# Weight sums on VectorE, doubled products in two stages, and attention's later sums in row 0

## The chip, the cores and the metric

The kernel runs on one core of a Trainium2 chip. The metric is device time in microseconds, as the median of several executions; a separate profiled execution gives the trace. TensorE (PE) multiplies matrices into PSUM, which here is split into eight banks of 128 x 512 float32. VectorE (DVE) and ScalarE (ACT) read PSUM and SBUF, GpSimd (POOL) works on SBUF and issues some transfers, SyncE (SP) issues the others. Each engine executes its own list of instructions strictly in order.

## The reference: one layer of a hybrid decoder

There are 512 tokens, a model width of 2048, and float32 throughout.

```
h = RMSNorm(x)
[u | v_sgu | q | k | v_att | g_a | g_b] = h @ W_in            # 2048 x 9216
y_a = gelu(u) * (tril(W_s) v_norm + b)                        # chunks of 128 tokens
y_b = stick-breaking attention, 8 heads of 128, blocks of 128 queries:
      z = q k^T * scale
      log_1m = where(key < query, log_sigmoid(-z), 0)
      tail   = sum of log_1m over the keys that come later
      w      = where(key < query, exp(log_sigmoid(z) + tail), 0);  y_b = w v
x += (sigmoid(g_a) * (y_a W_up_a) + sigmoid(g_b) * (y_b W_up_b)) @ W_o
x += (silu(gate) * up) @ W_ffn_out,   [gate | up] = RMSNorm(x) @ W_ffn_in   # hidden 5632
x += sigmoid(RMSNorm(x) @ W_pg) * (p @ W_ple)
```

## The kernel before

**Numbers.** TensorE's fast format, float32r, keeps fewer bits than float32. So each operand is split into a high and a low part, `hi = round(x)` on ACT (L313 for weights, L245 for activations) and `lo = x - hi` on VectorE (L310, L246). One float32 product is three float32r products: hi by hi, hi by lo, lo by hi. `mm3` issues them as three matmuls (L250, L251, L252).

**Seven products for eight.** Most matrices are multiplied in pairs of tiles: 256 x 256 weights against 256 rows of 512 tokens, seen as 2 x 2 blocks, with Strassen's scheme in Winograd's form ("S" units; "P" units are plain). It takes seven block products of 128 x 128 weights against 256 columns instead of eight. Seven weight blocks are needed: three land as they are, two are made by a transfer that adds while it writes (L317, issued on POOL's queue), and two are sums that POOL makes with two additions (L329) into a small buffer, `summed`.

**Preparing weights.** Class `Weights` does it in four steps for two units at a time: `landed` (the adding transfer), `high` (ACT, L313), `sums` (POOL, L329), `rest` (VectorE's L310, then L313 and L310 for the two sums). Three pairs of buffers `whi`/`wlo` (slots) hold the results and four landing buffers the raw weights. `in_turn` pins the order of these instructions and of the evictions on each engine; the remaining order is set by a list scheduler with its own estimates.

**Pairs.** A `Pair` accumulates one output block of 256 rows x 512 tokens over 8 units, two units at a time. In the first stage (33 of the 36 column blocks of `W_in`, and the attention and the gating beside them) products share banks: the seven halves `a, a, q, q, z, y, y` take four banks, with three 256-column matmuls for each product. In FFN-in (43 of 44 blocks) the pair is *doubled*: the stationary hi block meets [hi | lo] of the activations in one matmul of 512 columns (L589), then the lo block meets hi in one of 256 (L591). Each of the seven products then has a whole bank, hi part and lo part side by side: six banks of the pool `ps` and one of `small`. `mix` or `mix_doubled` evicts them while the last two units run. In `mix_doubled` the seven banks are p1, p6, p7, p5, p4, p2, p3 in the order of the products.

**Attention** runs beside the first stage, two heads per round, four rounds. For each head, and each block j of 128 keys from the last to the first, `stage_a` makes the logits and `stage_b` the sums: a triangular matrix of ones times the block's terms (L987, float32, up to 512 columns), plus all ones times `later`, the running sum of the later blocks (L989, float32). `later` is kept on POOL (L997) and VectorE (L999). L991 subtracts the result.

## Time and profile before

| | us |
|---|---|
| median of 3 runs (lowest, highest) | 2770.14 (2769.76, 2771.31) |
| span of the profiled execution | 2768.0 |
| that execution's time above its span | not recorded; the median lies 2.1 above the span |
| first stage with attention, about 110 to 846 | 736 |
| gated merge with W_up, 846 to 1213 | 367 |
| FFN-in, 1256 to 2109 | 853 |
| FFN-out, 2109 to 2490, and the last gate, 2490 to 2768 | 381 and 278 |

The stage bounds are read from where the lines of a stage begin and end in the trace. A timeline row gives start, duration, engine, line, what is written and read, shapes and count. Matmuls overlap in the pipeline: a matmul of 256 columns lasts 0.28 us in a row, but the next starts much sooner, so the cost of a matmul is the distance between two starts. In a row of grouped instructions the columns are busy time, mean duration of one, and idle time of the engine before them with what ended it. A few per cent of the matmul records are missing, so counts of matmuls are taken from the program.

### The profile page before, as it was taken

What the parts mean: (1) busy time and instruction counts of PE and PEld (TensorE: products, weight loads), DVE (VectorE), ACT (ScalarE), POOL (GpSimd) and SP (SyncE); (2) the same over time, 40 slices, a digit from 0 to 9 for tenths busy, and PEclk for the clock granted to TensorE, in tenths of its full rate; (3) what the DMA queues carried; (4) which work ended last, traced back from release to release, by engine and by line L of the source; (5) the groups of instructions that cost most, each with busy time, mean ns of one, the idle gap of its engine ahead of it and who ended that gap; (6) DMA issues with size and microseconds to landing.
All of it is one profiled execution on the core that took longest, in us unless ns stands there. A gap on an engine that the chain in (4) does not pass through costs nothing.

```text
span 2768.0 us, 46391 instructions
## 1 busy us (share of the span) xinstructions
PE 2709.9 (98%) x17243; PEld 2442.2 (88%) x17243; DVE 1922.3 (69%) x2581; ACT 1351.4 (49%) x2043; POOL 1203.9 (43%) x1321
## 2 busy tenths in 40 slices
PE   8999999999999999999999999999999999999999
PEld 6899999999999889978888888888887998988898
DVE  7565656565666566578788888878888457677766
ACT  7655556564554334365444444444445344444543
POOL 0455555555551012215656656665663323423232
PEclk9999999999999999999999999999999999999999
DMA  7567677667776447667878877887886668787785
GB/s 218 141 169 180 171 174 172 165 173 192 174 181 205 132 144 203 196 205 196 210 196 199 199 196 194 201 200 198 200 193 197 179 167 235 201 258 223 229 227 154
DMA packets 302851, 529.09 MB, mean 191 GB/s; under 512 B 25632, under 2 KB 162848, under 8 KB 302624
## 3 DMA queue, kind: packets, MB, share of 16 engines
q1 hardware_dynamic: 241872, 425.70, 48.7%
q0 software_dynamic: 60752, 100.43, 23.6%
q8 instruction: 135, 2.21, 0.3%
q14 instruction: 92, 0.75, 0.1%
HBM read 478.84 MB, written 47.19 MB: 190 GB/s over the span
## 4 chain that ended last, share of the span: by engine, by line
PE 79%; DVE 8%; DMA 4%; ACT 3%; issue 2%; POOL 2%; SPq 0%; DVEq 0%; ACTq 0%; POOLq 0%
PE ps L251 18%; PE ps L250 18%; PE ps L252 18%; PE ps L589 13%; PE ps L591 7%; DVE out L649 3%; DVE wlo L310 3%; PE small L589 2%; POOL wholes L329 2%; DMA wholes<-x 2%; PE small L591 1%; DMA wholes<-hid 1%; ACT whi L313 1%; DVE wholes L464 1%; DVE parts L246 1%
## 5 line engine op out<-in xcount | busy, mean ns | idle before, releaser
L313 ACT ACTIVATE whi<-wholes 128x512 fp32r<-128x512 f32 (+4 forms) x950 | 854.1, 917 | 975.2 <-POOL wholes L329 350.9
L310 DVE TENSOR_TENSOR wlo<-wholes,whi 128x512 fp32r<-128x512 f32 (+4 forms) x950 | 1039.1, 1117 | 388.0 <-ACT whi L313 384.2
L250 PE MATMUL ps<-parts,whi 128*128 128x256 f32 (+1 forms) x3995 | 1249.0, 315 | 24.9 <-ACT whi L313 13.3
L251 PE MATMUL ps<-parts,whi 128*128 128x256 f32 (+1 forms) x3960 | 1233.7, 312 | 3.4 <-DVE parts L246 3.4
L252 PE MATMUL ps<-parts,wlo 128*128 128x256 f32 (+1 forms) x3960 | 1231.0, 311 | 1.4 <-DVE wlo L310 1.4
L329 POOL TENSOR_TENSOR wholes<-wholes 128x256 f32<-128x256 f32 (+1 forms) x794 | 789.0, 994 | 760.0 <-DVE wlo L310 492.9
L250 PEld LDWEIGHTS ps<-parts,whi 128*128 128x128 f32 x3995 | 765.1, 192 | 74.2 <-ACT whi L313 14.2
L251 PEld LDWEIGHTS ps<-parts,whi 128*128 128x128 f32 x3960 | 759.1, 192 | 49.5 <-DVE parts L246 7.0
L252 PEld LDWEIGHTS ps<-parts,wlo 128*128 128x128 f32 x3960 | 758.3, 192 | 40.6 <-DVE wlo L310 2.5
L589 PE MATMUL ps<-parts,whi 128*128 128x512 f32 x2064 | 736.1, 397 | 7.0 <-DVE out L649 5.6
L591 PE MATMUL ps<-parts,wlo 128*128 128x256 f32 x2064 | 578.4, 280 | 0.0
L589 PEld LDWEIGHTS ps<-parts,whi 128*128 128x128 f32 x2064 | 387.2, 188 | 107.5 <-issue 18.5
L591 PEld LDWEIGHTS ps<-parts,wlo 128*128 128x128 f32 x2064 | 390.4, 189 | 0.0
L317 POOL DMA_DIRECT2D wholes<-w_ffn_in x172 | 152.1, 884 | 252.6 <-DMA wholes<-w_ffn_in 201.6
L317 POOL DMA_DIRECT2D wholes<-w_in x132 | 118.3, 900 | 188.3 <-DMA wholes<-w_in 186.1
L246 DVE TENSOR_TENSOR parts<-wholes,parts 128x1024 fp32r<-128x1024 f32 (+3 forms) x129 | 127.4, 1006 | 22.8 <-ACT parts L245 22.0
L649 DVE TENSOR_TENSOR out<-out,ps 128x256 f32<-128x256 f32 x258 | 106.5, 413 | 45.5 <-ACT out L646 44.7
L618 DVE TENSOR_TENSOR out<-out 128x256 f32<-128x256 f32 x59 | 25.8, 438 | 157.6 <-ACT out L615 157.6
L589 PE MATMUL small<-parts,whi 128*128 128x512 f32 x344 | 130.0, 395 | 0.0
L245 ACT ACTIVATE parts<-wholes 128x1024 fp32r<-128x1024 f32 (+3 forms) x129 | 105.9, 844 | 45.6 <-DMA wholes<-hid 21.3
L317 POOL DMA_DIRECT2D wholes<-w_ffn_out x56 | 57.8, 1043 | 94.0 <-DMA wholes<-w_ffn_out 47.9
L591 PE MATMUL small<-parts,wlo 128*128 128x256 f32 x344 | 96.4, 280 | 0.0
(119 smaller groups left out, 1646.8 us busy)
## 6 DMA issues: line engine op xcount, KB each, us to landing
wholes<-w_ffn_in SPq DMA_DIRECT2D x172, 384.0 KB, 5.1
wholes<-w_in SPq DMA_DIRECT2D x132, 384.0 KB, 4.7
wholes<-w_ffn_in SPq DMA_DIRECT2D x172, 256.0 KB, 4.4
wholes<-w_ffn_in POOLq DMA_DIRECT2D x172, 256.0 KB, 5.4
wholes<-w_in SPq DMA_DIRECT2D x132, 256.0 KB, 3.9
wholes<-w_in POOLq DMA_DIRECT2D x132, 256.0 KB, 4.5
wholes<-x SPq DMA_DIRECT2D x32, 512.0 KB, 5.5
wholes<-w_ffn_out SPq DMA_DIRECT2D x31, 512.0 KB, 3.8
```

What stands on the lines that cost most here:

```text
L245: return (nc.scalar.activation(hi, src, AF.Copy), nc.vector.tensor_tensor(out=lo, in0=src, in1=hi.bitcast(F32), op=ALU.subtract))
L246: nc.vector.tensor_tensor(out=lo, in0=src, in1=hi.bitcast(F32), op=ALU.subtract))
L250: nc.tensor.matmul(ps[:, s], sh, mh[:, s], start=start, stop=False)
L251: nc.tensor.matmul(ps, sh, ml, start=False, stop=False)
L252: return nc.tensor.matmul(ps, sl, mh, start=False, stop=stop)
L310: in_turn(nc.vector.tensor_tensor(out=self.lo[:, blocks], in0=r, in1=h.bitcast(F32), op=ALU.subtract))
L313: in_turn(nc.scalar.activation(h, r, AF.Copy))
L317: nc.gpsimd.dma_start(out=raw[:, 3:5], in_=self.src[:, 1:3], accum_op=ALU.add)
L329: in_turn(nc.gpsimd.tensor_tensor(out=o, in0=x, in1=y, op=ALU.add))
L589: nc.tensor.matmul(ps, wh[:, w], t[:, x].rearrange("p s c -> p (s c)"), start=first, stop=False)
L591: mark(nc.tensor.matmul(ps[:, :256], wl[:, w], t[:, x, 0], start=False, stop=last))
L649: in_turn(nc.vector.tensor_tensor(out=out, in0=x, in1=y, op=op))
```

## The change

1. The two sums of weight blocks move from POOL to VectorE (now L336), and their split into hi (ACT, now L320) is issued in the step `sums`, one step earlier than before.
2. `doubled` becomes a number. In the first stage five of the seven products are doubled, each in a bank of its own; the last two, p2 and p3, share one bank "r" with `mm3`. FFN-in keeps seven. Of the two units, the second runs its two matmuls in turned order (256 columns first, then 512), in `twice`, now L620.
3. `mix_doubled` adds p5 into two outputs with two 256-column instructions instead of one of 512, and reads both halves of a bank closer together.
4. Attention: row 0 of a strictly triangular matrix is empty, so it is filled with ones, and row 0 of the block's terms carries the sums of the later blocks. The row's own terms are saved in `own`. The product is now made in float32r, with the terms split into hi and lo (L246, L247), as two matmuls (L1024, L1025). The result's row 0 plus `own` becomes row 0 of the next block (L1027).
5. Buffers: two landing buffers of full and three of smaller size at the start, four full ones from the end of the plain first pairs; attention's tiles are taken later; two split tiles `sp0`, `sp1` are new.

```diff
-                        in_turn(nc.gpsimd.tensor_tensor(out=o, in0=x, in1=y, op=ALU.add))
+                        in_turn(nc.vector.tensor_tensor(out=o, in0=x, in1=y, op=ALU.add))
+                    split(False, slice(5, 7), s)
             def rest():
                 split(True, slice(0, c), raw)
                 if self.kind == "S":
-                    split(False, slice(5, 7), s)
                     split(True, slice(5, 7), s)
...
-                    if self.doubled:
-                        ps = self.at(i)
-                        nc.tensor.matmul(ps, wh[:, w], t[:, x].rearrange("p s c -> p (s c)"),
-                                         start=first, stop=False)
-                        mark(nc.tensor.matmul(ps[:, :256], wl[:, w], t[:, x, 0], start=False,
-                                              stop=last))
+                    if i < self.doubled:
+                        self.twice(self.at(i), wh[:, w], wl[:, w], t[:, x], first, last, u == 1)
+                    elif self.doubled:
+                        ps = self.at("r")[:, 256 * (i - 5) : 256 * (i - 4)]
+                        mark(mm3(ps, wh[:, w], wl[:, w], t[:, x, 0], t[:, x, 1],
+                                 first and i == 5, last and i == 6))
...
+        def twice(ps, wh, wl, x, first, last, turned):
+            steps = [(ps, wh, x.rearrange("p s c -> p (s c)")), (ps[:, :256], wl, x[:, 0])]
+            for k, (out, w, t) in enumerate(reversed(steps) if turned else steps):
+                i = nc.tensor.matmul(out, w, t, start=first and k == 0, stop=last and k == 1)
+            mark(i)
...
             copy(c22, p7[0])
+            tt(c22, c22, p7[1], add)
             tt(c12, c12, c11, add)
-            tt(c22, c22, p7[1], add)
             yield
             copy(s5, p5[0])
+            tt(s5, s5, p5[1], add)
             tt(c22, c22, c12, add)
-            tt(s5, s5, p5[1], add)
             yield
             tt(c21, c22, p4[0], add)
-            tt(b[:, 1:4:2], b[:, 1:4:2], s5.unsqueeze(1).to_broadcast([P, 2, 256]), add)
             tt(c21, c21, p4[1], add)
             yield
...
+                tt(c12, c12, s5, add)
+                yield
+                tt(o[:, :T], self.at("r"), o[:, :T], sub)
+            tt(c22, c22, s5, add)
...
+            own = a_tile("own", n, 3 * P if j == 2 else 0)[0:1] if j else None
+            if j > 0:
+                nc.vector.tensor_copy(own, zs[0:1])
+            nc.vector.memset(zs[0:1, :P], 0.0)
...
-            nc.tensor.matmul(tp, tri, sp, start=True, stop=j == NT - 1)
-            if j < NT - 1:
-                nc.tensor.matmul(tp[:, P:], ones, later[:, j * P :], start=False,
-                                 stop=True)
+            split_into(hi, lo, sp)
+            nc.tensor.matmul(tp, tri, hi, start=True, stop=False)
+            nc.tensor.matmul(tp, tri, lo, start=False, stop=True)
+            if j > 0:
+                nc.vector.tensor_tensor(out=state[h, j - 1][0][0:1, P:], in0=tp[0:1], in1=own,
+                                        op=ALU.add)
...
-            yield pair(xs, last=i == len(srcs) - 1, home=lambda: block(*order[i]))
+            yield pair(xs, last=i == len(srcs) - 1, home=lambda: block(*order[i]), doubled=5)
```

Three places show how the instructions move. In FFN-in, VectorE's list at the end of a pair, before (the `ps` banks numbered 1232 to 1236 are p1, p6, p7, p5, p4 of this pair):

```order
L649 TENSOR_TENSOR out_1239_17054<-out_1239_17054,ps_1232_16934 128x256
L649 TENSOR_TENSOR out_1239_17054<-out_1239_17054,ps_1233_16939 128x256
L649 TENSOR_TENSOR out_1239_17054<-out_1239_17054 128x256
L649 TENSOR_TENSOR out_1239_17054<-out_1239_17054,ps_1234_16944 128x256
L310 TENSOR_TENSOR wlo2_81<-wholes_74,whi2_80 128x1280
L310 TENSOR_TENSOR wlo2_81<-wholes_74,whi2_80 128x512
L649 TENSOR_TENSOR out_1239_17054<-out_1239_17054 128x256
L649 TENSOR_TENSOR p75_1240_17059<-p75_1240_17059,ps_1235_16955 128x256
L649 TENSOR_TENSOR out_1239_17054<-out_1239_17054,ps_1236_16962 128x256
L649 TENSOR_TENSOR out_1239_17054<-out_1239_17054,p75_1240_17059 128x2x256
L649 TENSOR_TENSOR out_1239_17054<-out_1239_17054,ps_1236_16962 128x256
```

The same place of the changed kernel, with the two sums of the next weights (L336) ahead of the evictions (banks 1258 to 1262 are p1, p6, p7, p5, p4):

```order
L336 TENSOR_TENSOR wholes_74<-wholes_74 128x256 x2
L666 TENSOR_TENSOR out_1265_15852<-out_1265_15852,ps_1258_15732 128x256
L666 TENSOR_TENSOR out_1265_15852<-out_1265_15852,ps_1259_15737 128x256
L666 TENSOR_TENSOR out_1265_15852<-out_1265_15852,ps_1260_15742 128x256
L666 TENSOR_TENSOR out_1265_15852<-out_1265_15852 128x256
L317 TENSOR_TENSOR wlo1_79<-wholes_74,whi1_78 128x1280
L317 TENSOR_TENSOR wlo1_79<-wholes_74,whi1_78 128x512
L666 TENSOR_TENSOR p75_1266_15857<-p75_1266_15857,ps_1261_15752 128x256
L666 TENSOR_TENSOR out_1265_15852<-out_1265_15852 128x256
L666 TENSOR_TENSOR out_1265_15852<-out_1265_15852,ps_1262_15759 128x256 x2
```

Between the lo splits and the second reading of p4's bank there was an instruction of 2 x 256 elements; now the two readings of p4 follow each other, and the work with p5 comes after them.

In the first stage, VectorE's list at the end of a pair in the changed kernel, while attention's last sum of a head is made (L247 splits the terms, L1029 needs TensorE's L1025; `ps_109` is the bank "r"):

```order
L666 TENSOR_TENSOR p75_120_1230<-p75_120_1230,ps_104_1058 128x256
L666 TENSOR_TENSOR out_119_1225<-out_119_1225 128x256
L247 TENSOR_TENSOR sp1_132<-wholes_74,sp0_131 128x512
L666 TENSOR_TENSOR out_119_1225<-out_119_1225,ps_108_1076 128x256 x2
L1029 TENSOR_TENSOR wholes_74<-wholes_74,small_121_1260 128x512
L666 TENSOR_TENSOR out_119_1225<-out_119_1225,p75_120_1230 128x256
L666 TENSOR_TENSOR out_119_1225<-ps_109_1081,out_119_1225 128x512
```

The eviction of bank "r" stands behind an instruction that waits for TensorE. TensorE's own list there, in the pair that follows:

```order
L620 MATMUL ps_127_1313<-parts_73,whi1_78 128x512
L620 MATMUL ps_127_1313<-parts_73,wlo1_79 128x256 x2
L620 MATMUL ps_127_1313<-parts_73,whi1_78 128x512
L620 MATMUL ps_124_1293<-parts_73,whi0_76 128x512
L1025 MATMUL small_121_1260<-sp1_132,tri_122 128x512
L620 MATMUL ps_124_1293<-parts_73,wlo0_77 128x256 x2
L620 MATMUL ps_124_1293<-parts_73,whi0_76 128x512
L620 MATMUL ps_125_1298<-parts_73,whi0_76 128x512
L620 MATMUL ps_130_1324<-parts_73,whi1_78 128x512
```

The list goes on to the next two units (`whi0`) before the fifth product of the first two (`ps_130`), and the low part of attention's sum (L1025) is placed among them. The two 256-column matmuls in the middle of a product are the turned order.

More of the change, by code (lines that the diff above doesn't have):

```diff
@@ L259, in hybrid_layer, with more_landings, fewer_landings @@
     summed = take(2 * 2 * P, "high")
-    def more_landings(n):
-        spare[0] += n
-        while spare[0] > 0:
-            spare[0] -= 1
-            landings.append(take(5 * 2 * P, "high"))
+    def more_landings(n, size=LANDING):
+        for _ in range(n):
+            landings.append(take(size, "high"))
+    def fewer_landings():
+        for x in [x for x in landings if x.n < LANDING]:
+            landings.remove(x)
+            give(x)
+        spare[0] = sum(-1 for x in prepared if x.land.n < LANDING)
     chain = {}
@@ L547, in __init__ @@
             self.both = all(self.n.values())
-            self.doubled = doubled and not self.n["P"]
+            self.doubled = 0 if self.n["P"] else doubled
             self.o, self.home, self.banks = None, home, {}
@@ L637, in mix_doubled @@
         def mix_doubled(self, o):
-            p1, p6, p7, p5, p4, p2, p3 = ((b[:, :256], b[:, 256:]) for b in map(self.at, range(7)))
+            full = [(b[:, :256], b[:, 256:]) for b in map(self.at, range(self.doubled))]
+            p1, p6, p7, p5, p4 = full[:5]
             b = o.rearrange("p (b c) -> p b c", c=256)
@@ L897, in hybrid_layer @@
     eps_cols = consts.tile([P, NT], F32, name="eps_cols")
+    sp_parts = [consts.tile([P, T], F32R, name=f"sp{i}") for i in range(2)]
     def flip(o):
@@ L1038, in attention @@
         if rnd == 3:
-            for tag in ("k", "v", "zs"):
+            for tag in ("k", "v", "zs", "own"):
                 give(att.pop(tag))
@@ L1071, in sgu_v @@
                 op0=ALU.mult, op1=ALU.add)
+        if rnd == 3:
+            for tag in list(att):
+                give(att.pop(tag))
     def scaled(o, row):
@@ L1094, in block @@
         if w == "s":
-            y_a[i] = take(1024)
+            y_a[i] = take(1024, "high")
             return y_a[i].f()
@@ L1263, in hybrid_layer @@
     for m in range(KH):
-        o = pair(fs, last=m == KH - 1, plain=m == 0, doubled=True).out()
+        o = pair(fs, last=m == KH - 1, plain=m == 0, doubled=7).out()
         if m == 0:
```

68 lines of the change are left out of this document (38 added, 30 removed).

## The prediction, made before the changed kernel was run

> **What bounds the kernel now.** I read the page first, then the windows of the stages, then TensorE's waits and its timeline.
>
> ```profile
> span 2768.0 us, 46391 instructions
> PE 2709.9 (98%) x17243; PEld 2442.2 (88%) x17243; DVE 1922.3 (69%) x2581; ACT 1351.4 (49%) x2043; POOL 1203.9 (43%) x1321
> ...
> 110.00:846.00 736.00, 725.71 (x5770) 701.34 (x5769) 451.41 (x577) 412.23 (x779) 402.83 (x498) 1.00 0.71 174
> 1256.00:2109.00 853.00, 845.39 (x4781) 730.12 (x4779) 692.57 (x990) 401.72 (x560) 514.00 (x505) 1.00 0.81 199
> 2109.00:2490.00 381.00, 372.75 (x2378) 339.46 (x2379) 246.98 (x339) 165.06 (x221) 123.30 (x142) 0.99 0.74 207
> ```
>
> TensorE is busy 98% of the span, at a granted clock of 1.00 in the two long stages. So the time is the number of matmuls times the distance between their starts, plus 58 us of idleness and the smaller waits that the pipeline covers up. An edit elsewhere is worth something only if it shortens TensorE's list or one of its waits. In a row of the windows the third busy time is VectorE's. It has room: 61% in the first stage (451.41 of 736), 81% in FFN-in (692.57 of 853), 65% in FFN-out (246.98 of 381).
>
> **Attention's sums, TensorE.** The last block of a head:
>
> ```profile
> 627.06 0.28 PE L252 MATMUL ps<-parts,wlo 128*128 128x256 f32 x1
> 627.18 1.02 PE L987 MATMUL small<-wholes,tri 128*128 128x512 f32 x2
> 628.04 0.81 PE L989 MATMUL small<-wholes,ones 128*128 128x384 f32 x2
> 628.39 0.58 PE L250 MATMUL ps<-parts,whi 128*128 128x256 f32 x1
> 628.80 0.28 PE L251 MATMUL ps<-parts,whi 128*128 128x256 f32 x1
> ...
> 1011.96 0.39 PE L250 MATMUL ps<-parts,whi 128*128 128x512 f32 x1
> 1012.64 0.39 PE L250 MATMUL ps<-parts,whi 128*128 128x512 f32 x1
> ```
>
> From the start of L987 to the second matmul after it are 1.62 us, of which 0.12 is the product between: 1.50 us for 512 + 384 float32 columns, 1.67 ns a column. A head has 1280 such columns in L987 and 768 in L989: 2048 x 1.67 ns = 3.43 us, 27.4 us for eight heads. The last two rows are three float32r matmuls of 512 columns apart: 0.227 us each; one of 256 takes 0.12 (rows below), so 0.174 for 384. New: two matmuls each of 512, 384 and 256 columns, 2 x (0.227 + 0.174 + 0.12) = 1.04 us a head, plus two of 128, a width that float32r has nowhere in the trace: between 0.06 (half of 256) and 0.21 us (128 float32 columns at 1.67 ns). That is 1.16 to 1.46 us a head, 9.3 to 11.7 us in all. Saved: 15.7 to 18.1, taken as **17 us**.
>
> **Doubled products.** Rows of the first stage, then of FFN-in:
>
> ```profile
> 602.10 0.28 PE L250 MATMUL ps<-parts,whi 128*128 128x256 f32 x1
> 605.22 0.28 PE L252 MATMUL ps<-parts,wlo 128*128 128x256 f32 x1
> ...
> 1277.17 0.39 PE L589 MATMUL ps<-parts,whi 128*128 128x512 f32 x1
> 1278.90 0.39 PE L589 MATMUL ps<-parts,whi 128*128 128x512 f32 x1
> ...
> 1599.95 0.40 PE L589 MATMUL ps<-parts,whi 128*128 128x512 f32 x1
> 1610.20 0.40 PE L589 MATMUL ps<-parts,whi 128*128 128x512 f32 x1
> ```
>
> The first two rows are 26 starts apart: 0.12 us a matmul, 0.36 a product. The next two are five products apart, 0.346 each; the last two 29 products, 0.353 each. A doubled product has two speeds: 0.346, which is just one 512 and one 256 (0.227 + 0.12), and 0.353. In the timeline TensorE keeps one speed until its next wait, then draws again. Doubling therefore saves 7 to 14 ns on 33 pairs x 8 units x 5 products = 1320 products: 9 to 18 us, taken as **13**, since both speeds are common.
>
> Turning the second unit's order puts 256 beside 256 and 512 beside 512 in half of the places, the neighbours that give 0.12 and 0.227 elsewhere. No row shows the mixed order, so it is worth 0 (the draw stays) to 7 ns (always the fast speed) of whichever products draw the slow one. On FFN-in's 43 x 56 = 2408 products, about half of them slow, that is 0 to 8 us: **3.5**.
>
> By the Trainium skill ("TensorE: Matmul & The Clock Gate", Wait — 56ns, not 53.3ns?) a matmul pays about 2.5 ns beside its columns; a matmul less per product would then save an estimated 3 us in the first stage, not 13. The rows above disagree: 256 columns take 0.12 us where that rule gives 0.109, and both speeds of the doubled product lie further below three matmuls than 2.5 ns.
>
> **FFN-in's wait.** Once in nearly every pair TensorE waits for an eviction:
>
> ```profile
> PE ps L589 <- DVE out L649: 5.6, 23, 0.7
> ...
> 1730.90 0.28 PE L591 MATMUL ps<-parts,wlo 128*128 128x256 f32 x1
> 1731.26 0.47 PE L589 MATMUL ps<-parts,whi 128*128 128x512 f32 x1
> ...
> 1728.41 0.42 DVE L649 TENSOR_TENSOR out<-out 128x256 f32<-128x256 f32 x1
> 1728.74 0.41 DVE L649 TENSOR_TENSOR p<-p,ps 128x256 f32<-128x256 f32 x1
> 1729.07 0.41 DVE L649 TENSOR_TENSOR out<-out,ps 128x256 f32<-128x256 f32 x1
> 1729.52 1.26 DVE L649 TENSOR_TENSOR out<-out,p 128x512 f32<-128x512 f32 x1
> 1730.70 0.41 DVE L649 TENSOR_TENSOR out<-out,ps 128x256 f32<-128x256 f32 x1
> ...
> 1291.76 0.47 PE L589 MATMUL ps<-parts,whi 128*128 128x512 f32 x1 [0.21 <-DVE out L649]
> 2090.09 0.47 PE L589 MATMUL ps<-parts,whi 128*128 128x512 f32 x1 [0.22 <-DVE out L649]
> ```
>
> TensorE wants p4's bank for the next pair at 1731.02 (1730.90 + 0.12) and gets it at 1731.26, after the second reading (1730.70). The view of waits shows only 5.6 us, because the pipeline's tail covers the start of each. The last two rows are the same place 40 pairs apart: 19.96 us a pair. At the fast speed 56 products take 19.4, at the slow one 19.8; with the two about equal the wait, with its slow restart, costs some 0.36 us. The change removes the 1.18 us between the readings (1729.52 to 1730.70). p4's bank should be free near 1730.1, 0.9 us ahead of need. 42 x 0.36 = **15 us**; the bounds are 0 (something else holds it) and 22 (all over 19.4, the draw included).
>
> What holds it otherwise is VectorE's list. Its new load in FFN-in, from starts:
>
> ```profile
> 1726.40 2.09 DVE L310 TENSOR_TENSOR wlo<-wholes,whi 128x1280 fp32r<-128x1280 f32 x2
> ...
> 1738.90 0.68 DVE L1258 TENSOR_TENSOR out<-out 128x512 f32<-128x512 f32 x1
> 1739.50 2.32 DVE L310 TENSOR_TENSOR wlo<-wholes,whi 128x1280 fp32r<-128x1280 f32 x1
> 1746.50 1.49 DVE L310 TENSOR_TENSOR wlo<-wholes,whi 128x1280 fp32r<-128x1280 f32 x1
> ...
> 1739.42 2.99 POOL L329 TENSOR_TENSOR wholes<-wholes 128x256 f32<-128x256 f32 x2
> ```
>
> Two lo splits (1280 and 512) take 2.01 us (1726.40 to 1728.41), a 256-column instruction 0.33 (1728.41, 1728.74, 1729.07). A pair: 4 x 2.01, 8 sums and 14 evictions at 0.33, two of 512 for the hidden product (0.60 each, 1738.90 to 1739.50): 8.0 + 7.3 + 1.2 = 16.5 us of some 19.5, 85%. That presumes the undisturbed split, 1.49 us; beside POOL's sum it took 2.32. If the long ones stayed, 4 x 0.8 us would make it full.
>
> The Trainium skill ("SBUF — State Buffer", Who interferes with whom) says that a VectorE instruction with two SBUF inputs and a GpSimd instruction that reads SBUF exclude each other. The last three rows above agree, and by that rule the long splits go with L329; if they had another cause, the second rival below would weigh more.
>
> **The sums' own place.**
>
> ```profile
> L329 POOL TENSOR_TENSOR wholes<-wholes 128x256 f32<-128x256 f32 x738 | 751.6, 1018 | 702.0 <-DVE wlo L310 464.7 <-DMA wholes<-w_ffn_out 66.9 <-DMA wholes<-w_in 41.8
> PE small L819 <- DVE diag L817: 5.7, 3, 3.3
> PE small L903 <- ACT wholes L925: 4.0, 4, 1.7
> PE small L964 <- DVE wholes L991: 1.0, 1, 1.0
> 92.76 1.03 POOL L329 TENSOR_TENSOR wholes<-wholes 128x256 f32<-128x256 f32 x1
> 93.45 1.34 POOL L852 TENSOR_TENSOR cols<-mean,expo 128x4 f32<-128x4 f32 x1
> ```
>
> 794 additions leave POOL. In the long stages they waited for L310, hardly for transfers, so on VectorE, right behind the same L310, they find their weights landed. POOL's adding transfers are no longer queued behind sums. Near 93 us TensorE waits 3.3 us for a norm whose power (L852) stood behind sums on POOL: **3 us** saved (0 to 5). In FFN-out the sums did wait for transfers (66.9 us); on VectorE such a wait holds up lo splits and evictions. VectorE is 65% busy there, so I charge **1 us** (-4 to 8).
>
> **New waits in the first stage.** All six `ps` banks belong to one pair, where before two were spare. Attention's splits wait for ACT and VectorE, and L1029 waits for TensorE ahead of bank "r"'s eviction. The list moves the next two units' products forward there, which covers about 2 us. Before, attention's transposes (L903) and logits (L964) made TensorE wait 4.0 and 1.0 us, 5 us in 33 pairs. The chain is now longer by two instructions and a bank, so I charge one and a half times as much on top, an estimate of 0.25 us a pair: **8 us** lost (0 to 50, at 1.5 us a pair).
>
> **The sum.** 2768.0 - 17 - 13 - 3.5 - 15 - 3 + 1 + 8 = 2725.5 for the profiled span; the median lies 2.1 above it: **2728 us**.
>
> **Rivals.** *FFN-in's wait stays* (20%): the sums and the split of ACT in front of the evictions push VectorE back by what the reorder gains. For: 85% load and a strict order. Against: 0.9 us of room. Then 15 us are not saved: 2743. *FFN-out waits for sums* (10%): of the 66.9 us a third reaches TensorE, 22 instead of 1: 2749. *The six banks decide* (8%): VectorE's list in the first stage, held by attention's waits, returns a bank late in every pair. The gains without that loss are 50.5 us, so the kernel becomes slower from 1.5 us a pair on; at 2 us, 66 instead of 8: 2786. For: L1029's place. Against: 61% load before, and lists that were laid out around it. *The doubling does nothing* (2%): the draw turns out slow and the switch between forms costs the rest: 2741. The forecast keeps 60%, with its own range of 2711 to 2738.
>
> Range, 8 in 10: 2710 to 2757. It leaves out the six banks and the best ends together. A difference of 0.2% (5.5 us) is what a measurement of this kernel can tell. Faster by more 0.89, within 0.03, slower 0.08.
>
> **What would show it.** Right: L1024 and L1025 together near 10 us; products of L620 spaced near 0.347; FFN-in pairs of 19.4 to 19.6 us, with no wait of TensorE for L666; no L317 split of 1280 columns over 1.6 us; first stage near 736 - 22 us. Wrong: TensorE waiting for L666 in the first stage or for L317 in FFN-in, VectorE waiting at L336 for transfers, L1024 of 128 columns far above 0.2 us.

## The result, and the profile after

The changed kernel takes **2753.72 us** (median of 4 executions, 2750.65 to 2762.71) against 2770.72 for the kernel before (4 executions, 2769.76 to 2776.52): ratio **0.9941**, 95% interval 0.9923 to 0.9960. It is 17 us faster. Forecast were 42, and 2728 us; the time lies in the range of 2710 to 2757, but more than half of the gain is missing.

To see where, both traces are cut at the same events: the first product of the first stage in halves of 256 columns or doubled, the first 512-column product of `W_up`, the first one of `W_o`, the last doubled product of FFN-in, the end. A row has start and end, length, then busy time of PE, PEld, DVE, ACT and POOL, the granted clock, the DMA share and GB/s. The kernel before:

```profile
90.90:861.70 770.80, 757.17 (x6018) 732.39 (x6019) 467.23 (x599) 430.46 (x815) 415.09 (x509) 1.00 0.70 173
861.70:1035.80 174.10, 174.10 (x770) 144.24 (x770) 111.99 (x115) 66.21 (x64) 8.10 (x7) 1.00 0.50 157
1035.80:2106.70 1070.90, 1057.99 (x6053) 919.24 (x6052) 836.59 (x1175) 509.00 (x698) 564.60 (x559) 1.00 0.78 199
2106.70:2768.00 661.30, 641.45 (x4077) 582.47 (x4075) 446.18 (x593) 285.90 (x381) 205.42 (x231) 0.99 0.74 208
```

The changed kernel, its page's head and the same four windows:

```profile
span 2760.9 us, 43150 instructions
PE 2691.6 (97%) x15875; PEld 2361.8 (86%) x15875; DVE 2167.8 (79%) x3713; ACT 1365.6 (49%) x2142; POOL 440.8 (16%) x503
...
88.40:852.30 763.90, 741.81 (x4651) 652.95 (x4651) 607.55 (x1154) 447.82 (x914) 190.84 (x225) 0.99 0.69 175
852.30:1027.10 174.80, 174.37 (x770) 144.07 (x769) 113.89 (x122) 66.86 (x63) 2.63 (x3) 1.00 0.50 160
1027.10:2082.40 1055.30, 1048.56 (x6052) 916.70 (x6051) 907.65 (x1587) 505.22 (x698) 164.50 (x187) 1.00 0.78 202
2082.40:2760.90 678.50, 648.12 (x4078) 583.95 (x4076) 479.72 (x749) 287.22 (x380) 78.18 (x77) 0.98 0.70 202
```

This profiled execution was the longest of its four. A second profile of the same kernel (run e14 below) stands beside it, so that no conclusion hangs on one execution:

| us | before | changed | changed, e14 | forecast of the change |
|---|---|---|---|---|
| start to the first stage | 90.9 | 88.4 | 88.0 | 0 |
| first stage | 770.8 | 763.9 | 761.6 | -25 |
| `W_up` | 174.1 | 174.8 | 175.0 | 0 |
| `W_o` and FFN-in | 1070.9 | 1055.3 | 1051.3 | -18.5 |
| FFN-out and the gate | 661.3 | 678.5 | 679.1 | +1 |
| span | 2768.0 | 2760.9 | 2755.0 | -42.5 |

(The first stage's forecast is -17 - 13 - 3 + 8, that of FFN-in -15 - 3.5. The -3 is POOL's norm, whose wait of 3.3 us ends in the kernel before at 95.63 us, so behind the boundary at 90.90.) FFN-in came as forecast, and the start, which had no term, gained 2.5 to 2.9 us. The first stage gained 7 to 9 us of 25, and behind FFN-in 17 to 18 us were **lost** where 1 was allowed for. These two stretches are nearly the whole error.

TensorE's waits in the first stage, in the kernel before and in the changed one, then behind FFN-in, in the same order (us in total, times, longest):

```profile
PE small L1065 <- ACT wholes L925: 5.3, 4, 1.3
PE small L903 <- ACT wholes L925: 4.0, 4, 1.7
PE small L819 <- DVE diag L817: 3.3, 1, 3.3
PE small L964 <- DVE wholes L991: 1.0, 1, 1.0
```
```profile
PE small L1040 <- POOL wholes L1031: 5.7, 5, 3.0
PE ps L620 <- DVE wholes L666: 4.5, 2, 3.1
PE small L1094 <- ACT wholes L955: 3.7, 3, 2.8
PE small L933 <- ACT wholes L955: 3.0, 2, 1.7
```
```profile
PE ps L250 <- ACT parts L245: 6.4, 3, 3.4
PE ps L250 <- ACT whi L313: 2.7, 1, 2.7
PE ps L251 <- DVE parts L246: 1.7, 3, 0.8
```
```profile
PE ps L251 <- ACT parts L246: 6.7, 3, 2.9
PE ps L251 <- ACT whi L320: 4.4, 6, 1.1
PE ps L252 <- DVE parts L247: 4.3, 4, 2.2
PE ps L251 <- ACT parts L459: 3.4, 3, 2.5
```

(The changed kernel's L246, L247, L320, L459, L666, L933 and L1094 are L245, L246, L313, L451, L649, L903 and L1065 of before.) In the first stage two waits are new: TensorE stands at L1040, a head's last products, for POOL's masking, and twice for an eviction into `wholes`. Behind FFN-in it stands longer for the splits of activations (`parts`) and for those of weights (`whi`). Waits are not the whole loss there: of the 17.2 us in this profile 10.5 are idle time of TensorE, and 6.7 are busy time for the same matmuls. TensorE's granted clock is 0.5 for 24 us of this stretch, against 14 us before.

**The y store.** The larger of the two evictions, in time:

```profile
344.88 0.33 SPq L1044 DMA_DIRECT2D y<-wholes  x1
...
349.21 0.94 ACT L663 ACTIVATE wholes<-ps 128x256 f32<-128x256 f32 x3 [4.35 <-DMA y<-wholes]
...
349.63 1.08 DVE L666 TENSOR_TENSOR wholes<-wholes,ps 128x256 f32<-128x256 f32 x3 [8.32 <-ACT wholes L663]
...
350.10 0.50 PE L620 MATMUL ps<-parts,whi 128*128 128x512 f32 x1 [3.06 <-DVE wholes L666]
```

A q pair's result goes into the block from which the previous round's y has just been sent to memory. The store was issued at 344.88 when attention ended; ACT's first copy of the pair waited for it 4.35 us; VectorE waited for ACT, and TensorE for the bank. In the kernel before the same copy stood behind its product, not behind the store, which had been issued 2.97 us ahead of it (now the store takes 4.3; the four stores of the kernel before landed in 2.8 in the median):

```profile
354.82 0.33 SPq L1015 DMA_DIRECT2D y<-wholes  x1
...
357.79 0.60 ACT L615 ACTIVATE wholes<-ps 128x512 f32<-128x512 f32 x1 [1.01 <-PE ps L252]
...
y<-wholes SPq DMA_DIRECT2D x4, 512.0 KB, 2.8
```

**Half clock behind a wait.** After some waits TensorE ran about 3.4 us at a clock of 0.5. These windows are behind the transposes of the same q pair (they end a wait of 1.7 us at 368.3), and the 3.4 us that follow:

```profile
368.90:372.30 3.40, 3.40 (x13) 2.93 (x12) 1.36 (x4) 2.24 (x6) 0.95 (x1) 0.51 0.73 126
372.40:375.80 3.40, 3.40 (x26) 3.21 (x25) 3.26 (x7) 2.32 (x6) 0.00 (x0) 1.00 0.17 47
```

Thirteen matmuls instead of 26: 1.7 us lost on top of the wait. The changed kernel has three such windows between 98 us and the end of the first stage, the kernel before none. The other two follow waits of L1040 (3.0 us, at 450) and L1094 (2.8 us, at 675). Not every wait has one behind it: after the 3.06 us that end at 350.10 the clock stayed at 1.00, while in e14's profile the wait at the same place (3.2 us) was followed by one.

### The profile page after: what moved, and what is told of

Read it like the earlier page. It is cut to its first block, busy times and chain, and to the rows that moved or that the text cites. A ratio compares the mean times of both kernels' runs of the same rounds, so it can differ in the third digit from the quotient of the medians.

```text
span 2760.9 us, 43150 instructions
## 1 busy us (share of the span) xinstructions
PE 2691.6 (97%) x15875; PEld 2361.8 (86%) x15875; DVE 2167.8 (79%) x3713; ACT 1365.6 (49%) x2142; POOL 440.8 (16%) x503
## 4 chain that ended last, share of the span: by engine, by line
PE 83%; DVE 7%; DMA 4%; ACT 3%; issue 2%; POOL 2%; SPq 0%; DVEq 0%; ACTq 0%; POOLq 0%
PE ps L620 36%; PE ps L252 13%; PE ps L251 13%; PE ps L253 13%; PE small L620 4%; DVE wlo L317 3%; ACT whi L320 1%; DMA wholes<-hid 1%; DVE out L666 1%; DMA wholes<-w_in 1%; PE small L1040 1%; DMA wholes<-x 1%; DVE wholes L336 1%; DVE parts L247 1%; PE small L933 1%
## 5 line engine op out<-in xcount | busy, mean ns | idle before, releaser
L320 ACT ACTIVATE whi<-wholes 128x512 fp32r<-128x512 f32 (+4 forms) x950 | 848.4, 917 | 835.7 <-PE ps L252 325.7
L620 PE MATMUL ps<-parts,whi 128*128 128x512 f32 x3384 | 1132.5, 399 | 7.8 <-DVE wholes L666 4.5
L317 DVE TENSOR_TENSOR wlo<-wholes,whi 128x512 fp32r<-128x512 f32 (+4 forms) x950 | 961.4, 1045 | 111.6 <-ACT whi L320 110.8
L251 PE MATMUL ps<-parts,whi 128*128 128x256 f32 (+1 forms) x2675 | 857.3, 324 | 25.7 <-ACT whi L320 14.1
L252 PE MATMUL ps<-parts,whi 128*128 128x256 f32 (+1 forms) x2640 | 859.0, 326 | 4.4 <-DVE parts L247 4.3
L253 PE MATMUL ps<-parts,wlo 128*128 128x256 f32 (+1 forms) x2640 | 854.0, 325 | 2.2 <-DVE wlo L317 2.2
L620 PEld LDWEIGHTS ps<-parts,wlo 128*128 128x128 f32 x3384 | 636.0, 188 | 143.8 <-DVE wlo L317 2.0
L620 PE MATMUL ps<-parts,wlo 128*128 128x256 f32 x3384 | 673.1, 280 | 1.2 <-DVE wlo L317 1.2
L251 PEld LDWEIGHTS ps<-parts,whi 128*128 128x128 f32 x2675 | 509.5, 191 | 74.5 <-ACT whi L320 17.2
L620 PEld LDWEIGHTS ps<-parts,whi 128*128 128x128 f32 x3384 | 544.9, 189 | 15.9 <-DVE wholes L666 5.0
L252 PEld LDWEIGHTS ps<-parts,whi 128*128 128x128 f32 x2640 | 504.0, 191 | 52.1 <-DVE parts L247 7.1
L253 PEld LDWEIGHTS ps<-parts,wlo 128*128 128x128 f32 x2640 | 502.9, 191 | 42.5 <-DVE wlo L317 3.8
L336 DVE TENSOR_TENSOR wholes<-wholes 128x256 f32<-128x256 f32 (+1 forms) x794 | 328.0, 413 | 26.7 <-DMA wholes<-w_ffn_in 4.5
L666 DVE TENSOR_TENSOR out<-out,ps 128x256 f32<-128x256 f32 x373 | 151.9, 419 | 113.5 <-ACT out L663 103.2
L247 DVE TENSOR_TENSOR parts<-wholes,parts 128x256 fp32r<-128x256 f32 (+3 forms) x129 | 122.2, 965 | 29.7 <-ACT parts L246 29.5
L620 PE MATMUL small<-parts,whi 128*128 128x512 f32 x344 | 136.1, 396 | 0.0
L246 ACT ACTIVATE parts<-wholes 128x1024 fp32r<-128x1024 f32 (+3 forms) x129 | 106.3, 846 | 56.2 <-DMA wholes<-hid 24.9
L1290 ACT ACTIVATE out<-out 128x512 f32<-128x512 f32 x44 | 27.9, 635 | 190.8 <-DVE out L1289 190.8
```

The costliest lines, as they stand in the source:

```text
L246: return (nc.scalar.activation(hi, src, AF.Copy), nc.vector.tensor_tensor(out=lo, in0=src, in1=hi.bitcast(F32), op=ALU.subtract))
L247: nc.vector.tensor_tensor(out=lo, in0=src, in1=hi.bitcast(F32), op=ALU.subtract))
L251: nc.tensor.matmul(ps[:, s], sh, mh[:, s], start=start, stop=False)
L252: nc.tensor.matmul(ps, sh, ml, start=False, stop=False)
L253: return nc.tensor.matmul(ps, sl, mh, start=False, stop=stop)
L317: in_turn(nc.vector.tensor_tensor(out=self.lo[:, blocks], in0=r, in1=h.bitcast(F32), op=ALU.subtract))
```

## The experiments

All medians stand beside runs of the kernel before on the same chip (2769 to 2772 us). e1 to e4 ran on one chip, and so did e5 to e8, e9 to e12 and e13 to e16; differences of 2 or 3 us between these groups say nothing. "Pooled" is the median of the ten executions of the changed kernel that were timed here, 2756.2.

### The y store: e1 and e2

```diff
-        if w == "q":
-            y_b[i] = take(1024)
-            return y_b[i].f()
...
+            if h == 0:
+                y_b[i] = take(1024)
...
-            nc.scalar.activation(s, flip(q.f()), AF.Copy, ...)
+            nc.scalar.activation(y_b[i].f(h * T, h * T + T), flip(q.f()), AF.Copy, ...)
```

> The changed kernel, but a q pair's result is evicted into scratch, and the block that holds q and later y is taken only when q is written back into it, some 10 us later. What the kernel computes is the same. Theory (late store): in the changed kernel's profile the first eviction of two of the three later q pairs stood behind the store of the previous round's y, since attention ends later while the doubled pair's evictions begin earlier; TensorE stood 3.2 us at 350 and 1.7 us at 497, and 1.9 and 1.4 us more at the transposes that follow. Without that wait the first stage (728 us from 110 to 838) falls to 719 to 723 and the median from 2753.7 to 2745 to 2749. Rival (covered): what waits there has other work in front of it, and the delay only moves to attention's own waits: first stage 726 to 730, median 2751 to 2756.

Measured: 2747.54 us, ratio 0.9928 (0.9912 to 0.9945). The first stage took 753.1 us instead of 763.9. The waits of L620 for `wholes` are gone, and so are those of the transposes (L933); L1040's stayed (4.8 us). The theory holds for the median. The half-clock window at 368.9 is gone too; two are in the profile, at 579 and 732, at waits of L1040 and L1094 again.

e2 adds one number, two places more ahead of `finish`, which issues L1040:

```diff
             stage_b(h, 0)
-            yield 2
+            yield 4
             finish(h)
```

> As e1, and a head's last products (L1040) two places later in the list, so that the chain sum, subtraction, exp, masking on POOL has some 5 us more. Theory (chain too long for its place): the five waits of L1040 for POOL's masking (6.5 us in the changed kernel's profile, and about 3 us more at a lower granted clock behind the 3.2 us one at 450) go: 5 to 9 us less than e1, median 2738 to 2743. Rival: the later products meet the next head's logits and small banks, so the wait moves to L996 or L1024: within 2 us of e1.

Measured: 2745.49 us, ratio 0.9914 (0.9901 to 0.9927). The profile has no wait of L1040 for POOL and no half clock between 42 us and the end of the first stage, which is 24 us shorter than before the change:

```profile
89.40:836.00 746.60, 736.18 (x4652) 649.01 (x4651) 608.57 (x1153) 445.60 (x914) 203.31 (x225) 1.00 0.72 179
```

Against e1 the median fell by 2 us only, less than the 5 to 9 expected and what the rival had said; this profile was the fastest of e2's four executions (2739.8; the others 2744.9 to 2746.3), so its stretch flatters somewhat. The waits are as the theory says; how much of the 6.5 us between the two profiled stages the median holds is within the scatter. (e6 and e16 below have the same first stage; it took 745.1 and 747.0 us.)

### The sums in the mixed stages: e3

```diff
-                        in_turn(nc.vector.tensor_tensor(out=o, in0=x, in1=y, op=ALU.add))
-                    split(False, slice(5, 7), s)
+                        e = nc.gpsimd if self.pool else nc.vector
+                        in_turn(e.tensor_tensor(out=o, in0=x, in1=y, op=ALU.add))
+                    if not self.pool:
+                        split(False, slice(5, 7), s)
...
-            plan(w_o[j], OUT)
+            plan(w_o[j], OUT, 0, True)
```

> The changed kernel with the two weight sums back on POOL, and their hi split behind the others on ACT, in the stages that mix Strassen and plain units (w_o, FFN-out, the gate); the first stage and FFN-in keep the sums on VectorE. Theory (my second rival, sums on VectorE wait for transfers there and hold up splits and evictions): FFN-out and the gate, 385 + 291 us in the changed kernel's profile against 381 + 278 before, go back to about 660, the waits for parts and whi/wlo to some 23 us from 41, and the median falls by 10 to 17 us, to 2737 to 2744. Rival (that profile fell on an execution 10 us above the others, and the sums' place matters little there): the stages come out at 660 to 676 either way and the median within 4 us of 2753.7.

Measured: 2768.24 us (11 executions), ratio 0.9992 (0.9981 to 1.0003): 12 us above the pooled time, not below. FFN-out and the gate took 685.9 us. So the sums on VectorE are no cause of the loss there; they make it smaller. My second rival falls, and the cause was still to be found.

### The scratch: e5 and e7

The whole diff has one line that the excerpt above does not show and that I gave no term: `WHOLES = 13824` became 13200, the columns of F32 scratch from which blocks are taken. An activation's *form* (its Strassen sums and hi/lo split) is begun at the first place of the program where its blocks fit. The order in which the program issues its work shows it, counted in places between units (1013 in all): at place 843 the kernel before has six forms left to begin, the changed kernel seven; at place 955, in the gate, none against four.

e5 lends the place of attention's two split tiles, free after the first stage, to blocks of up to 1024 columns:

```diff
+    sp_scope.close()
+    more = ctx.enter_context(tc.tile_pool(name="more", bufs=1))
+    wholes.more = Arena("more", 2 * T, F32, more.tile([P, 2 * T], F32, name="more"))
...
+            if self.more and n <= 1024 and how != "place":
+                try:
+                    return self.more.take(n)
+                except ValueError:
+                    pass
```

> The changed kernel, whose F32 scratch (wholes) is 13200 columns instead of 13824, gets 1024 columns more from the end of the first stage on: the two hi/lo tiles of attention's sums are given up there and their place is lent to blocks of up to 1024 columns. Theory (small scratch): an activation's form is begun only when its blocks fit, and with 624 columns less the plain and Strassen forms of w_o, FFN-out and the gate are begun 1 to 4 places (of some 2.6 us) later, so that TensorE waits for parts and lo splits; with the room back, the stretch behind FFN-in falls from 672.7 us to 645 to 658 (655.6 before the change) and the median from 2753.7 to 2732 to 2740. Rival (VectorE and ACT are simply later there, whatever the room): 665 to 675 us and 2749 to 2757.

Measured: 2748.62 us, ratio 0.9926 (0.9907 to 0.9944). At place 955 no form is left to begin; at 843 there are still seven. FFN-out and the gate went back to the time of before, to 1 us, but the median fell by 8 us only, to the edge of the rival's range:

```profile
2089.00:2751.40 662.40, 641.53 (x4078) 581.52 (x4076) 479.81 (x749) 287.56 (x380) 78.14 (x77) 0.99 0.74 208
```

e7 is the reverse, one line in the kernel *before*, at the end of the first stage:

```diff
+    take(624, "high")
```

> The kernel before, from which 624 columns of wholes are taken for good at the end of the first stage; nothing else differs. Theory (small scratch): the forms of w_o, FFN-out and the gate are then begun at the very places of the changed kernel, and since the sums are still on POOL, as in e3, the stretch behind FFN-in grows from 655.6 to some 675 to 682 us (680.2 in e3): median 2785 to 2796, 16 to 26 above before. Rival (the room does not matter): within 5 us of before.

Measured: 2798.48 us, ratio **1.0103** (1.0086 to 1.0119): 27 us slower from 624 columns of scratch alone. In the stages behind, the forms are then begun at the very places of the changed kernel (seven left at 843, four at 955). The last window and TensorE's waits in it (the profiled execution was the longest of six):

```profile
2114.70:2802.30 687.60, 647.05 (x4077) 583.03 (x4075) 448.36 (x592) 284.41 (x381) 217.18 (x231) 0.98 0.71 199
```
```profile
PE ps L250 <- ACT parts L245: 12.6, 5, 6.7
PE ps L250 <- ACT whi L313: 7.3, 6, 3.4
PE small L819 <- DVE diag L817: 5.3, 1, 5.3
PE ps L252 <- DVE wlo L310: 3.4, 5, 1.1
```

The wait for ACT's splits of activations doubled (6.4 before), as a form begun late must show. With the sums on VectorE the way is less clear: from the changed kernel to e5 TensorE's idle time in this stretch fell from 30.4 to 20.9 us, yet the waits for the splits of activations hardly changed (14.4 and 13.7 us); the waits for ACT's splits of weights fell from 4.4 to 0.7 us. That the room is the cause is shown, which of the late forms costs the time is not. FFN-out and the gate in four combinations:

| FFN-out and the gate, us | sums on POOL | sums on VectorE |
|---|---|---|
| room for the forms | 661.3 (before) | 661.5 to 666.4, mean 663.5 (e5, e6, e12, e15, e16) |
| 624 columns less | 687.6 (e7), 685.9 (e3) | 672.4 to 679.1, mean 675.6 (changed, e1, e2, e4, e8 to e11, e13, e14) |

The scratch costs 25 to 26 us with the sums on POOL, 12 on the average with them on VectorE; the changed kernel's two profiles, 678.5 and 679.1, are the longest of their ten. In medians the room is worth 7 us (e5 and e15 against the changed kernel) and 10 (e6 against e2). Where the sums stand matters mainly where the forms are late.

### The six banks: e4 and e8

```diff
-            yield pair(xs, ..., home=lambda: block(*order[i]), doubled=5)
+            yield pair(xs, ..., home=lambda: block(*order[i]))
```

> The changed kernel with the first stage's seven products all in three matmuls of 256 columns again, as before the change, so that two banks are spare; attention, sums on VectorE and FFN-in stay as changed. Theory (the first stage's new waits come from attention's longer chain and the y store, not from the six banks): the products alone cost 1320 x 10.2 ns = 13.5 us more, the stage's TensorE stalls stay above 40 us (50 in the changed kernel, 29.5 before), median 2763 to 2769. Rival (banks): stalls go back to about 30 us, the stage grows by nothing or shrinks: median 2743 to 2755.

Measured: 2753.08 us, ratio 0.9944 (0.9930 to 0.9957), first stage 765.0 us: no loss. Here the rival is right. TensorE is idle 14.0 us of the stage (765.0 less 751.04 busy) where the changed kernel's idles 22.1 (763.90 less 741.81). The store is late all the same, but nobody waits behind it: ACT stands 4.36 us for it at 351 us, and L620's wait for L666 is not among TensorE's waits, since two more banks are spare.

```profile
351.29 0.60 ACT L631 ACTIVATE wholes<-ps 128x512 f32<-128x512 f32 x1 [4.36 <-DMA y<-wholes]
```

e8 makes the same edit in e2, where the store is out of the way:

> e2 with the first stage's products all in three matmuls of 256 again. e4 showed no loss against the changed kernel (2753.1 against 2753.7) though its products need 13.5 us more. Theory (the doubling is worth 13.5 us, and waits for the y store and behind attention's lists took it back): without those waits the loss shows: 2745.5 + 10 to 14 = 2755 to 2760. Rival (the six banks themselves cost what the doubling saves): within 4 us of e2.

Measured: 2748.29 us, ratio 0.9921 (0.9906 to 0.9937). The profiled first stage is 759.4 us against e2's 746.6: 12.8 us, the doubling's 13; TensorE's busy time in it is 12.1 us longer. But the medians lie only 2.8 apart, as the rival said, on two chips whose kernels before are 2.3 apart the same way, and e2's was the lucky profile. So what the doubling is worth once the store is mended, up to 13 us, stays open; before that it is worth nothing.

### Attention alone: e9

The float32 sums of before in the changed kernel (`tri` and `ones`, `later`, old `stage_a` and `stage_b`, 384 columns of scratch for 640):

```diff
-            split_into(hi, lo, sp)
-            nc.tensor.matmul(tp, tri, hi, start=True, stop=False)
-            nc.tensor.matmul(tp, tri, lo, start=False, stop=True)
+            nc.tensor.matmul(tp, tri, sp, start=True, stop=j == NT - 1)
+            if j < NT - 1:
+                nc.tensor.matmul(tp[:, P:], ones, later[:, j * P :], start=False, stop=True)
```

> The changed kernel with attention's sums as before the change (float32 products with tri and ones, the running sum of later blocks); doubling, sums on VectorE, FFN-in and the scratch of 13200 columns stay as changed. Theory (the new sums save 15 us of TensorE's list, 27.4 against 12, but their longer chain brings as much in waits: outside the gaps between records the first stage's stalls grew from 13 to 31 us, and three stretches of half clock behind them cost 5 more): undone, the first stage stays within 5 us of 764 and the median within 5 us of 2753.7. Rival (the six banks made those waits, attention only shows them): the stalls stay near 30 us and the 15 us come on top: first stage 775 to 782, median 2765 to 2772.

Measured: 2762.05 us, ratio 0.9964 (0.9952 to 0.9977), 6 us above the pooled changed kernel; first stage 769.5. Between the two theories: of the 14 us that the new sums take off TensorE's list (from start to start the old ones take 27.7 us in the trace of before, the new ones 13.4 in that of the changed kernel), about 6 arrive. The wait for the store is 0.4 us here, so it is the new chain that makes the store late. But L1040's wait (L1039 here) is there with the old sums too, and longer:

```profile
PE small L1039 <- POOL wholes L1030: 9.3, 7, 2.3
```

It was not among the waits of the kernel before, and the sums here are the old ones, so the new sums are not its cause. What is left is the new work of VectorE in this stage (585.72 us in e9 for 467.23 before); in e4, without the doubling, the same wait was 2.5 us. No run takes that work away alone, so this cause is likely and not shown.

### FFN-in's wait: e10 and e13

e10 is e3's switch, set for FFN-in alone:

```diff
-            plan(w_ffn_in[m], ("S" if m else "P") * KU)
+            plan(w_ffn_in[m], ("S" if m else "P") * KU, 0, True)
```

> The changed kernel with the weight sums of FFN-in alone back on POOL. Theory (the order of the evictions ended FFN-in's wait): TensorE still waits less than 1.5 us in all for p4's bank (L666), the long lo splits come back (mean above 1.1 us for 1280 columns beside POOL's sums), and w_o with FFN-in (1055.2 us in the changed kernel's profile, 1071.0 before) stays below 1060. Rival (VectorE reached the second reading of p4 late because POOL's sums lengthened its splits): the wait for L666 comes back and the two stages take 1066 to 1074 us.

Measured: 2792.25 us, ratio 1.0068 (1.0048 to 1.0087): 36 us above the pooled changed kernel, slower than before the change, with the new order of the evictions in place. `W_o` and FFN-in took 1082.3 us, beyond the rival's 1066 to 1074. In FFN-in, ACT's wait in the kernel before and in e10, then TensorE's in e10, and one instance:

```profile
ACT whi L313 <- POOL wholes L329: 218.2, 101, 3.5
```
```profile
ACT whi L321 <- POOL wholes L338: 320.6, 167, 4.2
```
```profile
PE ps L625 <- DVE out L671: 14.3, 24, 1.5
```
```profile
1325.97 1.80 ACT L321 ACTIVATE whi<-wholes 128x512 fp32r<-128x512 f32 x2 [2.74 <-POOL wholes L338]
1327.67 0.91 ACT L668 ACTIVATE out<-ps 128x256 f32<-128x256 f32 x3
...
1328.06 1.08 DVE L671 TENSOR_TENSOR out<-out,ps 128x256 f32<-128x256 f32 x3 [0.74 <-ACT out L668]
...
1334.22 0.47 PE L625 MATMUL ps<-parts,whi 128*128 128x512 f32 x1 [0.68 <-DVE out L671]
```

ACT stands 2.74 us at the hi split of a sum that POOL has not finished; the pair's first copies (L668) are queued behind that split, VectorE's evictions behind the copies, and some evictions later TensorE waits for a bank. My theory falls, the rival holds in direction: the sums' leaving POOL ended the wait. Why the wait for evictions is 14.3 us here and was 5.6 before the change was not found. The long lo splits came back too, in the groups by shape (1280 columns, mean ns): e10, then the changed kernel:

```profile
L318 DVE TENSOR_TENSOR wlo<-wholes,whi 128x1280 fp32r<-128x1280 f32 x164 | 300.1, 1830 | 1.6 <-ACT whi L321 1.1 <-DMA wholes<-w_ffn_in 0.5
```
```profile
L317 DVE TENSOR_TENSOR wlo<-wholes,whi 128x1280 fp32r<-128x1280 f32 x168 | 249.4, 1485 | 0.0
```

By the Trainium skill ("SBUF — State Buffer", Who interferes with whom) a VectorE instruction with two SBUF inputs contends with a GpSimd instruction that reads SBUF. The traces agree: 1830 ns with the sums on POOL, 1485 without.

e13 leaves the sums on VectorE and gives FFN-in's evictions the whole order of the kernel before; its main part is the broadcast addition back between the two readings of p4:

```diff
...
+                tt(c21, c22, p4[0], add)
+                tt(b[:, 1:4:2], b[:, 1:4:2], s5.unsqueeze(1).to_broadcast([P, 2, 256]), add)
+                tt(c21, c21, p4[1], add)
...
```

> The changed kernel with FFN-in's evictions in the order of the kernel before (a broadcast addition between the two readings of p4's bank); sums on VectorE, turned products and all else as changed. Theory (the order matters, as predicted): TensorE waits for that bank in most pairs again, w_o and FFN-in together grow from 1052 to 1055 us by 6 to 15. Rival (the sums on VectorE, with shorter lo splits and no hi split on ACT that waits for POOL, ended the wait, and the order adds nothing): within 3 us, with less than 3 us of waits for L666.

Measured: 2761.51 us, ratio 0.9966 (0.9950 to 0.9981). The stretch with FFN-in took 1053.5 us, as in the changed kernel, and no wait of TensorE for L666 is left in it. So the order is not needed for that. Yet the median is 5 us above the pooled changed kernel; the profile puts the difference in the first stage (766.7), whose list is the same (see e15).

### Turned order: e11

```diff
-   self.twice(self.at(i), wh[:, w], wl[:, w], t[:, x], first, last, u == 1)
+   self.twice(self.at(i), wh[:, w], wl[:, w], t[:, x], first, last, False)
```

> The changed kernel with every doubled product's 512 ahead of its 256, none turned. Theory (the turned order takes away the slow one of two speeds, 0.3467 and 0.3533 us a product, and one product of a turned pair takes 0.3484): FFN-in, 2408 products, grows by 0 to 6 us from its 855 to 859 us, with both speeds to be seen again, and the first stage by up to 3; median 2754 to 2760. Rival (turning is worth nothing): FFN-in within 1 us, products all near 0.348.

Measured: 2771.95 us (11 executions), ratio 1.0002 (0.9991 to 1.0014): 16 us lost, outside what either side expected. Rows of FFN-in, 29 products apart in e11, 18 apart in the changed kernel (a row with x2 starts with the second matmul of a turned product):

```profile
1599.82 0.40 PE L620 MATMUL ps<-parts,whi 128*128 128x512 f32 x1
...
1610.06 0.40 PE L620 MATMUL ps<-parts,whi 128*128 128x512 f32 x1
```
```profile
1599.74 0.63 PE L620 MATMUL ps<-parts,whi 128*128 128x512 f32 x2
...
1606.01 0.63 PE L620 MATMUL ps<-parts,whi 128*128 128x512 f32 x2
```

0.353 us a product against 0.348. Unturned, in this profile, TensorE keeps the slow speed from its last wait, some nine pairs into FFN-in, to the end of the stage; there is no wait left to draw again. The stretch took 1062.1 us in the profile, 7 to 11 more than the changed kernel's two. The rest of the 16 us is not located.

### Both mended, and one step more: e6, e12, and the repeats

e6 is e2 and e5 together.

> e2 (q in scratch first, a head's last products two places later) and e5 together. If the two losses are separate, their gains add: 2745.5 - 14 to 20 = 2725 to 2732. If one time lost only hides another, it stays above 2738.

Measured: **2735.72 us**, ratio 0.9869 (0.9849 to 0.9889); profiled first stage 745.1, FFN-out and the gate 661.5. The gains add, to 4 us above the range expected.

e12 splits attention's row sums one place earlier in e6; here for one of the four blocks:

```diff
-            split_into(hi, lo, sp)
...
+            stage_s(h, 2)
             stage_a(h, 1)
             yield 1
             stage_b(h, 2)
```

(`stage_s` holds the `split_into` taken out of `stage_b`.)

> e6 with the hi/lo split of attention's row sums one place (some 2.6 us) ahead of the products that read it. In e2's profile TensorE waited 7.2 us for these splits (L1028 4.2 for ACT, L1029 3.0 for VectorE). Theory: those waits go and nothing takes their place: 4 to 7 us less than e6, median 2729 to 2732. Rival (row 0, which the split needs, is not written by then, so the split blocks ACT and VectorE ahead of evictions): 0 to 5 us more than e6.

Measured: 2733.83 us, ratio 0.9866 (0.9842 to 0.9890): no difference from e6. In its profile, the longest of its four executions, the products wait longer for ACT's split than in e6 (10.9 us, 1.1 there), and the first stage took 757.2 us. That is the rival's sign, but not in the median; why the split is late was not shown.

```profile
PE small L1039 <- ACT sp L252: 10.9, 7, 3.5
```

Three runs repeat kernels side by side.

> The changed kernel itself once more, beside e15 and e16, so that the three are compared on one chip: 2750 to 2757 by what was seen; the stretch behind FFN-in 666 to 673 us.

Measured: 2756.37 us, ratio 0.9953 (0.9937 to 0.9968).

> e5 once more. Theory (the room is worth what its stretch shows, 13 to 16 us, and e5's first stage fell badly by chance): 11 to 16 us below e14. Rival (e5's median was right, and another part loses some of it): 3 to 7 us below e14.

Measured: 2751.05 us, ratio 0.9925 (0.9905 to 0.9945), 5 us below e14: the rival's figure again. With e5, twelve executions have a median of 2749.2, 7 below the pooled changed kernel, though the stretch itself is 15 to 17 us shorter in both profiles. Both also show a longer first stage (770.9 and 767.8) than the changed kernel's two (763.9 and 761.6). But seven profiles have the same first stage on VectorE, ACT and POOL, instruction for instruction (changed, e3, e5, e10, e13, e14, e15), and it took 758.7 to 770.9 us, 765.3 in the mean. So this is scatter between executions; what sets it was not found. Against it, the mended first stage of e2, e6 and e16 took 745.1 to 747.0.

> e6 once more: 2733 to 2737, so 16 to 21 us below e14, if the parts add as e2 and e6 showed.

Measured: **2732.29 us**, ratio 0.9865 (0.9852 to 0.9879), 24 us below e14: the same as e6. This version beats both kernels.

## Why the prediction was half right

**Attention's sums, 17 us.** Right in kind, and nearly in size on TensorE's list: 27.7 us became 13.4, so 14. In the changed kernel it is worth 6 us (e9); the longer chain makes the y store late.

**Doubling, 13 us.** TensorE's busy time fell by 12 us (e8 against e2), but in the changed kernel it is worth nothing (e4): with all six banks in one pair a late eviction stops TensorE, which with two spare banks it does not.

**New waits in the first stage, 8 us: the term that failed.** I scaled waits of before by one and a half and spread them over the pairs. Most of them sit at two places, the block that q and y share, and L1040's place in the list. Both were to be seen: the rows at 354.82 and 357.79 leave 2.97 us between the store's issue and the next copy into its block, and the list gives the finish two places after the last sums. With 7 to 9 us gained of 33 (17 + 13 + 3) the term was 24 to 26 us instead of 8. With both places mended (e2, e6, e16) the stage fell by 24 to 26 us, what the other three terms and the 8 had promised, 25. The rival of the six banks named the place where the loss would show, TensorE waiting for L666, but had it in every pair and at another price.

**FFN-in, 18.5 us.** The sum was right (15.6 and 19.6 us), but by luck: its reasons were not, and of its two parts one was too large and the other too small. The wait ended because the sums left POOL and with them ACT's place behind POOL (e10), not by the order of the readings (e13). The turned order, 3.5 us in the sum and 8 at most, is worth 7 to 11 there (e11): I took "half of the products slow" from a kernel that drew its speed anew after a wait in nearly every pair, and the change removes those waits. With 7 to 11 for the turned order, some 5 to 13 us are left for the wait that was to give 15.

**POOL's norm, 3 us.** Right: its wait of 3.3 us near 93 us is gone, and so are the 3.4 us at a clock of 0.5 behind it:

```profile
95.63 0.80 PE L819 MATMUL small<-diag,ones 128*128 128x128 f32 x2 [3.32 <-DVE diag L817]
```

It lies in the first stage. That the stage starts 2.5 to 2.9 us sooner is another gain, which had no term; no run shows its cause.

**FFN-out, 1 us.** Right for what it was meant for (661.5 to 666.4 with room, 661.3 before), and the rival of sums that wait for transfers fell: VectorE waited for them at L336 some 6 us in the whole program. But the line with the size of `wholes`, which stands in the whole diff, had **no term at all**. It cost 12 us on the average of the profiles and 7 to 10 in medians; the rest of the 17 to 18 is the scatter of the two executions profiled. I asked of each edited instruction what it costs, and not of an edited size what was begun by it.

Against the sum's span of 2725.5 us, e14's profile is 29.5 us longer: 15.8 in the first stage and 16.8 behind FFN-in, less 2.9 at the start; the rest came as forecast to 1 us each. Mended in both, the kernel takes 2732 to 2736.

## What to carry to other kernels

A change in the size of a pool is a change in the order of work wherever the program starts something when its memory fits: compare where the work is begun, far from the edit too. When a buffer is used again by the next round, look at how much time lies between its last transfer and the first write of its next owner; an edit that lengthens the one and hastens the other turns a margin of nothing into a wait. And when an edit removes the waits of a stage, take the speed that the engine keeps without them, not the mean that the waits had mixed.

## What the runs showed of the hardware

A 512-column and a 256-column matmul in turn have more than one steady speed, 0.347 and 0.353 us a pair, kept until the next wait in these traces. In e11 one spell of 0.353 lasted some 35 pairs of FFN-in; with the order of every second product turned the pitch was 0.348 through nearly all of it.

Some waits of TensorE of 1.7 to 3.2 us were followed by about 3.4 us, in places two or three times that, at a granted clock of 0.50 to 0.51 in which half as many matmuls started, so that a wait of 3 us followed by 3.4 us of it costs nearly 5. Others were not: after 3.06 us at 350 the clock stayed at 1.00.
